# The ninth feature pair moves into the block products of the FFN down projection

## The chip, the cores and the metric

One core of a Trainium2 chip runs one encoder layer as one launch. The metric is device microseconds of an execution; the kernel before takes 2078.09 us (median of three runs, 2076.51 to 2078.81). The engines are TensorE (PE, matmuls; PEld is its weight load), VectorE (DVE), ScalarE (ACT), GpSimd (POOL) and SyncE (SP), which issues every load and store of the kernel on one queue. The 16 DMA engines carry them out.

## The reference, cut to what matters

```python
D_MODEL, SEQ, DEC_SEQ, D_FF = 1024, 1024, 32, 2816
def swiglu(h, w_gate, w_up, w_down):
    return (jax.nn.silu(h @ w_gate) * (h @ w_up)) @ w_down
def layer(x, lw, sb_fn, s0, gla_chunk):
    x = x + 0.5 * swiglu(rmsnorm(x, g_ffn1), w1g, w1u, w1d)
    mix, k, v, s = token_mixer(rmsnorm(x, g_mix), ...)
    x = x + mix
    x = x + 0.5 * swiglu(rmsnorm(x, g_ffn2), w2g, w2u, w2d)
    return rmsnorm(x, g_final), k, v, s
```

The prompt's 1024 rows and the sample's 32 are computed together: 1056 columns when x is held transposed. The change touches `@ w_down` of both FFNs, and what the gate/up stage hands to it.

## The kernel before, in words

Everything is held transposed: x is eight tiles x[0] to x[7] of 128 features by 1056 columns. Float32 operands are split into a high and a low float32r half, and each product is three matmuls (high x high, high x low, low x high). D_FF is 22 tiles of 128, taken as 11 pairs (0,1), (2,3), ... named 0 to 10.

**Block products.** Large products are done by a Strassen-Winograd scheme: operands are cut in 2x2 blocks, and seven products of sums of blocks replace eight. `PRODUCTS` names for each of the seven which weight form (A11, S2, ...) meets which moving form (B11, T2, ...) in which of four PSUM accumulators a to d; `ORDER` = (1, 6, 7, 5, 2, 4, 3) is the order in which they run. Products 5 and 3 share accumulator d, so VectorE must have read product 5's result before product 3 accumulates.

**Gate and up** (`gate_up`, L473 for its matmuls). Twenty steps t, two a pair, each of seven products. After each product the loop calls slots: `Slots.split` puts the copy to a high half (ACT, L50) and the subtraction of the low half (DVE, L51) in the slots k and k+1 later, and a store in slot k+2. The finished hidden pair lies in x[4] to x[7]. For the pairs that the block products of the down stage will use, `form` makes the seven moving forms out of it (B11, T1, T2 and so on; the T forms by a subtraction), and `keep` splits each in x[0] or x[1] in turn and stores it in the DRAM tensor `part_spill` (528 KB a form). Each pair's forms are spread over the two or three steps behind it. Pairs listed in `PLAIN` are stored unsplit in `hid_spill` or, if in `SPLIT`, split in `hid_split`.

**Down.** Two parts. `Down.strassen` runs groups of two pairs; a group has four steps (`DownStep`), one for each 256 output features, a step has seven products, and a product has 2 column quarters x 2 pairs x 3 matmuls of 264 columns (L822). Behind each product a result is added to x on VectorE (L811) and GpSimd (L840). Before: four groups, pairs 1 to 8. Moving operands come from `part_spill` into 14 places of h and X, two sets of 14 in turn. A step's weights are loaded raw, and `first` and `second` make the sums on GpSimd (L799 among them) and the splits. `Down.plain` then does the six tiles in `PLAIN` (pairs 0, 9, 10) as ordinary products, in three chunks of 352 columns in the first FFN and four of 264 in the second, with the next norm done beneath it (`mix_norm` and `final`).

**The hand-over.** `Down.head` runs in the last gate/up step (t = 19), product by product: it issues the loads of group 0's parts, of the first weights and of x[0] to x[3], which had been lent out as scratch (x[0] and x[1] for `keep`, x[2] and x[3] for other splits). x[4] to x[7] follow during steps 0 and 1.

**What sets the order.** On the five engines the order around the change is fixed by hand (`manual_schedule`) in these stages; SyncE is in order too. Each transfer counts on one of eight semaphores in turn, so an issue also waits for the transfer eight issues ahead.

## Time and profile before

| what | value |
|---|---|
| median of three runs | 2078.09 us (2076.51 to 2078.81) |
| time of the profiled execution | 2074.93 us |
| its span | 2073.1 us |
| mean granted TensorE clock | 0.947 |
| TensorE busy | 2030.5 us, 98% |
| VectorE, ScalarE, GpSimd busy | 67%, 43%, 32% |
| block products, first and second FFN | 481.2 to 647.6 us, 1825.6 to 1989.6 us |
| plain products, second FFN, start | 1990.4 us |

A line of the profile names the source line, the engine, the operation, the tile written and those read (`pd_d<-part,whl`), the shape, the count, the busy time and mean ns, and then in the idle time before it what ended that. Numbers of buffers are left out, so `part`, `h` and `x` each stand for several tiles. `x<-x` on SyncE is a load of x from the input in the first FFN, `x<-x_spill` the same in the second. A line of the stretch table gives the stretch, its length, then busy time and count for PE, PEld, DVE, ACT and POOL, then granted clock, DMA share and GB/s.

### The profile page before, as it was taken

To read this page: it belongs to the slowest core of one execution; us is meant where nothing else is said; L and a number is where in the kernel's file an instruction comes from. 1 tells how busy PE (TensorE), PEld (TensorE's weight loads), DVE (VectorE), ACT (ScalarE), POOL (GpSimd) and SP (SyncE) were. 2 spreads that over 40 slices of the span, in tenths; PEclk is the share of its full clock that TensorE was granted. 3 is DMA by queue.
4 is the path that set the end of the run, shared out by engine and by line. 5 is a ranking of instruction groups with operands and counts; after the bars stand their busy time and mean duration, and the time that the engine had idled before them with its cause. 6 is when DMAs were issued, how large, how long until landed. Compare 5 with 4: busy or idle time off the path is not lost.

```text
span 2073.1 us, 39052 instructions
## 1 busy us (share of the span) xinstructions
PE 2030.5 (98%) x15746; PEld 1975.2 (95%) x15746; DVE 1386.0 (67%) x2166; ACT 883.3 (43%) x1630; POOL 671.2 (32%) x554
## 2 busy tenths in 40 slices
PE   7999999999999999999999999999999999999998
PEld 6999999999999988988999998999999999999997
DVE  6877777765677657386555477695775666566654
ACT  6444444442223443336555575454443333322233
POOL 0144434436774200121222200002433343367720
PEclk9999999999999999999999999999999999999998
DMA  6267676769863111111314152332673333498631
GB/s 234 104 235 262 244 249 248 267 225 395 319 241 111 61 62 62 65 63 53 106 58 122 59 183 92 112 96 89 237 251 141 140 148 143 148 398 317 220 120 67
DMA packets 142132, 349.83 MB, mean 169 GB/s; under 512 B 13176, under 2 KB 37144, under 8 KB 138368
## 3 DMA queue, kind: packets, MB, share of 16 engines
q1 hardware_dynamic: 141376, 346.80, 46.9%
q8 instruction: 124, 2.03, 0.4%
q10 hardware_dynamic: 576, 0.54, 0.1%
q14 instruction: 56, 0.46, 0.1%
HBM read 216.96 MB, written 124.65 MB: 165 GB/s over the span
## 4 chain that ended last, share of the span: by engine, by line
PE 89%; DVE 5%; ACT 3%; DMA 1%; issue 1%; SPq 0%; POOL 0%; DVEq 0%; ACTq 0%
PE acc_a L473 11%; PE acc_c L473 11%; PE acc_d L473 11%; PE acc_b L473 6%; PE pd_d L822 4%; PE pd_a L822 4%; PE pd_c L822 4%; PE pj L118 4%; PE acc L381 4%; PE pj L119 4%; PE pj L120 4%; PE pd L118 2%; PE pd L120 2%; PE pd L119 2%; PE pd_b L822 2%; PE av L1652 2%
## 5 line engine op out<-in xcount | busy, mean ns | idle before, releaser
L473 PE MATMUL acc_a<-h,whl 128*128 128x264 f32 x1920 | 247.9, 285 | 0.3 <-DVE whl L51 0.3
L473 PE MATMUL acc_d<-part,S 128*128 128x264 f32 x1920 | 246.3, 284 | 0.0
L473 PEld LDWEIGHTS acc_a<-h,whl 128*128 128x128 f32 x1920 | 239.5, 189 | 0.5 <-DVE whl L51 0.5
L473 PEld LDWEIGHTS acc_d<-part,S 128*128 128x128 f32 x1920 | 238.5, 188 | 0.1
L118 PE MATMUL pj<-h,whl 128*128 128x352 f32 x576 | 203.0, 352 | 0.0
L120 PE MATMUL pj<-h,whl 128*128 128x352 f32 x576 | 188.7, 328 | 0.0
L119 PE MATMUL pj<-h,whl 128*128 128x352 f32 x576 | 187.7, 326 | 0.0
L51 DVE TENSOR_TENSOR x<-x 128x528 fp32r<-128x528 f32 (+1 forms) x188 | 155.8, 844 | 19.0 <-ACT x L50 19.0
L50 ACT ACTIVATE x<-x 128x528 fp32r<-128x528 f32 (+1 forms) x188 | 117.3, 634 | 119.5 <-DVE x L546 30.3
L526 POOL TENSOR_TENSOR x<-tc,x 128x528 f32<-128x528 f32 x60 | 100.3, 1672 | 184.2 <-DVE tc L525 147.2
L444 POOL TENSOR_TENSOR s<-wraw 128x512 f32<-128x512 f32 x38 | 60.9, 1601 | 230.1 <-DVE S L113 164.2
L473 PE MATMUL acc_c<-h,A 128*128 128x264 f32 x960 | 124.3, 285 | 0.6 <-DVE u L492 0.6
L473 PE MATMUL acc_b<-h,S 128*128 128x264 f32 x960 | 124.2, 285 | 0.0
L473 PE MATMUL acc_c<-part,S 128*128 128x264 f32 x960 | 123.1, 284 | 0.0
L473 PEld LDWEIGHTS acc_c<-h,A 128*128 128x128 f32 x960 | 120.4, 188 | 0.8 <-issue 0.8
L473 PEld LDWEIGHTS acc_b<-h,S 128*128 128x128 f32 x960 | 120.4, 188 | 0.0
L1628 DVE TENSOR_TENSOR_SCAN w<-f,w 128x128 f32<-128x128 f32 (+3 forms) x64 | 86.8, 1357 | 49.2 <-ACT w L1626 48.9
L473 PEld LDWEIGHTS acc_c<-part,S 128*128 128x128 f32 x960 | 119.3, 188 | 0.0
L1046 POOL TENSOR_TENSOR nr<-nv,mhalf 128x18 f32<-128x18 f32 (+1 forms) x15 | 46.3, 3086 | 219.2 <-DVE nv L1044 199.3
L118 PEld LDWEIGHTS pj<-h,whl 128*128 128x128 f32 x576 | 109.2, 190 | 5.5 <-issue 2.6
L51 DVE TENSOR_TENSOR S<-s,S 128x512 fp32r<-128x512 f32 x152 | 113.9, 750 | 0.6 <-ACT S L50 0.6
L840 POOL TENSOR_TENSOR x<-x,u 128x528 f32<-128x528 f32 x64 | 98.2, 1553 | 45.1 <-DVE x L811 45.1
(407 smaller groups left out, 4885.2 us busy)
## 6 DMA issues: line engine op xcount, KB each, us to landing
part_spill<-x SPq DMA_DIRECT2D x112, 528.0 KB, 3.8
h<-part_spill SPq DMA_DIRECT2D x64, 528.0 KB, 10.7
part<-part_spill SPq DMA_DIRECT2D x48, 528.0 KB, 10.8
win_split<-x SPq DMA_DIRECT2D x44, 512.0 KB, 3.4
whl<-win_split SPq DMA_DIRECT2D x22, 1024.0 KB, 5.0
wraw<-w1g SPq DMA_DIRECT2D x22, 512.0 KB, 5.2
wraw<-w1u SPq DMA_DIRECT2D x22, 512.0 KB, 6.1
x<-win SPq DMA_DIRECT2D x44, 256.0 KB, 3.0
```

The source lines that it names most:

```text
L50: self.later(k, lambda: nc.scalar.activation(hi, src, AF.Copy))
L51: self.later(k + 1, lambda: nc.vector.tensor_sub(lo, src, hi.bitcast(F32)))
L118: nc.tensor.matmul(out, w[:, 0, wsl], a[:, 0, asl], start=first, stop=False)
L119: nc.tensor.matmul(out, w[:, 0, wsl], a[:, 1, asl], start=False, stop=False)
L120: nc.tensor.matmul(out, w[:, 1, wsl], a[:, 0, asl], start=False, stop=last)
L381: nc.tensor.matmul(out, self.w[i](k, a), quarter(S, k, b, j), start=k == 0 and n == 0, stop=k == KT - 1 and n == 2)
L444: eng.tensor_add(self.s1, a21, a22)
L473: nc.tensor.matmul(t[:, s, :SW], w[:, a, ks], m(k, b, s), start=fresh and k == 0 and n == 0, stop=k == 3 and n == 2, skip_group_check=not ...
L526: nc.gpsimd.tensor_mul(two(hid), t, sg)
L822: nc.tensor.matmul(t[:, s, :SW], w[:, u, k * P : k * P + P], b[:, v, ss(s)], start=fresh and k == 0 and i == 0, stop=k == 1 and i == 2, sk ...
L840: nc.gpsimd.tensor_add(x[r][h], x[r][h], u)
L1628: nc.vector.tensor_tensor_scan(wr, f[:, :L][:, ::-1], wr, 0.0, op0=ALU.mult, op1=ALU.add)
```

## The change

Pair 9 (hidden tiles 18 and 19) leaves the plain list and joins the block products. Groups are now (1, 2), (3, 4), (5, 6, 7), (8, 9): group 2 has three pairs, so its products have 18 matmuls, and a step needs the weights of a third pair (`third`, `load_third`). The two sets of 14 places become a ring of 28, in which each group takes the places behind the group before it; a table made in `Down.__init__` says behind which product each part is loaded. The plain list keeps four tiles and four weight slabs instead of six and six. `form` stores seven forms of pair 9 where it stored four split halves, and since the last of them are now made in step t = 19, in x[0] and x[1], `head` loads x[0] ahead of part 6 and x[1] one product later.

```diff
@@ -525,18 +525,12 @@
                 nc.vector.tensor_add(t, u, ps)
                 nc.gpsimd.tensor_mul(two(hid), t, sg)
             f, h = 2 * self.i + q // 2, q % 2
-            if f in PLAIN and f not in SPLIT:
+            if f in PLAIN:
                 nc.sync.dma_start(S.hidden[PLAIN.index(f)][:, h * HALF : h * HALF + HALF], hid)
 
     def form(self, name):
 
         b11, b12, b21, b22 = (self.S.x[4 + q][:, :HALF] for q in range(4))
-        if 2 * self.i in SPLIT:
-            q = {"B11": 0, "T1": 1, "B21": 2, "B22": 3}.get(name)
-            if q is not None:
-                out = self.S.hid2[PLAIN.index(2 * self.i + q // 2)][:, :, q % 2 * HALF : q % 2 * HALF + HALF]
-                self.keep(out, self.S.x[4 + q][:, :HALF])
-            return
         if 2 * self.i in PLAIN:
             return
         if name[0] == "B":
...
@@ -763,9 +758,9 @@
 
 
 
-PAIRS = [(1, 2), (3, 4), (5, 6), (7, 8)]
-PLAIN = (0, 1, 18, 19, 20, 21)
-SPLIT = (18, 19)
+PAIRS = [(1, 2), (3, 4), (5, 6, 7), (8, 9)]
+THREE = 2
+PLAIN = (0, 1, 20, 21)
 
 
 class DownStep:
...
@@ -803,6 +798,29 @@
         self.W = {"A11": cut(self.wa, 0), "A12": cut(self.wa, 1), "A22": cut(self.wb, 0)}
         self.W.update({f"S{i + 1}": cut(self.ws, i) for i in range(4)})
 
+    def third(self, raw):
+
+        S, nc = self.S, self.S.nc
+        a11, a22, a21, a12 = (raw[:, i * P : i * P + P] for i in range(4))
+        wide, one = self.D.third
+        pair = self.wb[:, :, 2 * P :]
+
+        def sums():
+            nc.gpsimd.tensor_add(a22, a21, a22)
+            nc.gpsimd.tensor_sub(a21, a11, a21)
+            nc.gpsimd.tensor_sub(a11, a22, a11)
+
+        split = lambda w, src, k: S.slots.split(w[:, 0], w[:, 1], src, k)
+        cut = lambda t, i: t[:, :, i * P : i * P + P]
+        split(pair, raw[:, : 2 * P], 1)
+        S.slots.later(3, sums)
+        split(wide[:, :, : 3 * P], raw[:, : 3 * P], 4)
+        split(cut(wide, 3), a12, 5)
+        S.slots.later(7, lambda: nc.gpsimd.tensor_sub(a12, a12, a11))
+        split(one, a12, 8)
+        self.W3 = {"A11": cut(pair, 0), "A22": cut(pair, 1), "S4": one}
+        self.W3.update({n: cut(wide, i) for i, n in enumerate(("S2", "S1", "S3", "A12"))})
+
     def emit(self, between):
         S, nc = self.S, self.S.nc
         acc = {}
...
@@ -815,13 +833,15 @@
             if fresh:
                 acc[role] = S.ps.tile([P, 2, 512], F32, name="pd_" + role, tag="acc")
             t, w = acc[role], self.W[wn]
+            ks = len(PAIRS[self.g])
             for s in range(2):
-                for k in range(2):
+                for k in range(ks):
                     b = self.D.part(self.g, n, k)
+                    wk = w[:, :, k * P : k * P + P] if k < 2 else self.W3[wn]
                     for i, (u, v) in enumerate(((0, 0), (0, 1), (1, 0))):
                         nc.tensor.matmul(
-                            t[:, s, :SW], w[:, u, k * P : k * P + P], b[:, v, ss(s)],
-                            start=fresh and k == 0 and i == 0, stop=k == 1 and i == 2, skip_group_check=not fresh,
+                            t[:, s, :SW], wk[:, u], b[:, v, ss(s)],
+                            start=fresh and k == 0 and i == 0, stop=k == ks - 1 and i == 2, skip_group_check=not fresh,
                         )
             ps = t[:, :, :SW]
             if p == 1:
...
@@ -851,21 +871,40 @@
         h, X = S.h, S.X
         h0 = lambda d: h[d][:, :, :HALF]
         h1 = lambda d: h[d][:, :, HALF:]
-        self.places = [
-            [h0(0), h0(1), h0(2), h0(3), h1(0), h1(1), h1(2), h1(3)] + X[:6],
-            X[6:] + [h0(4), h0(5), h0(6), h0(7), h1(4), h1(5), h1(6), h1(7)],
-        ]
-        self.tiles = S.h[:4] + S.XX[:2]
+        self.ring = [f(d) for f in (h0, h1) for d in range(4)] + X + [f(d) for f in (h0, h1) for d in range(4, 8)]
+        self.base = [7 * sum(len(p) for p in PAIRS[:g]) for g in range(len(PAIRS))]
+        self.tiles = S.XX[: len(PLAIN)]
         self.ws = []
         self.steps = [DownStep(self, g, m) for g in range(len(PAIRS)) for m in range(4)]
-        self.raw = {}
+        self.raw, self.raw3 = {}, {}
+        self.loads = {}
+        for g in range(1, len(PAIRS)):
+            before, ks = len(PAIRS[g - 1]), len(PAIRS[g])
+            early = len(self.ring) - 7 * before
+            for i in range(7 * ks):
+                if i < early:
+                    m, n = divmod(i * 7 // min(early, 7 * ks), 2)
+                    n *= 2
+                else:
+                    m, n = 3, (i - early) // before + 1
+                self.loads.setdefault((4 * (g - 1) + m, n), []).append((g, *divmod(i, ks)))
 
     def part(self, g, n, k):
-        return self.places[g % 2][2 * n + k]
+        return self.ring[(self.base[g] + n * len(PAIRS[g]) + k) % len(self.ring)]
+
+    def load_one(self, g, n, k):
+        self.S.nc.sync.dma_start(self.part(g, n, k).bitcast(F32), self.S.parts[PAIRS[g][k] - 1, n])
 
     def load_part(self, g, n):
-        for k, i in enumerate(PAIRS[g]):
-            self.S.nc.sync.dma_start(self.part(g, n, k).bitcast(F32), self.S.parts[i - 1, n])
+        for k in range(len(PAIRS[g])):
+            self.load_one(g, n, k)
+
+    def load_third(self, i):
+        pool, name = (self.S.raw2, "wraw2") if i == 0 else (self.S.raw, "wraw")
+        t = pool.tile([P, 1024], F32, name=name, tag=name)
+        self.S.nc.sync.dma_start(t, self.src[len(self.steps) + i])
+        for m in range(2):
+            self.raw3[4 * THREE + 2 * i + m] = t[:, m * 512 : m * 512 + 512]
 
     def load_step(self, i):
         if i < len(self.steps):
...
@@ -888,10 +927,11 @@
             self.load_part(0, 5)
             self.steps[0].first(self.raw.pop(0), 1)
         elif p == 5:
+            self.S.nc.sync.dma_start(self.S.x[0], xd[0])
+            self.load_part(0, 6)
+            self.steps[0].second(1)
+        elif p == 4:
             self.S.nc.sync.dma_start(self.S.x[1], xd[1])
-            self.load_part(0, 6)
-            self.S.nc.sync.dma_start(self.S.x[0], xd[0])
-            self.steps[0].second(1)
         elif p == 3:
             self.load_step(2)
             for d in (2, 3):
...
@@ -923,14 +964,16 @@
                             self.steps[i + 1].first(self.raw.pop(i + 1), 1)
                         if n == 1:
                             self.steps[i + 1].second(2)
-                    if st.g < last and n % 2 == 0 and 4 * (n // 2) + st.m < 7:
-                        self.load_part(st.g + 1, 4 * (n // 2) + st.m)
+                        if n == 0 and self.steps[i + 1].g == THREE:
+                            self.steps[i + 1].third(self.raw3.pop(i + 1))
+                    for x in self.loads.get((i, n), ()):
+                        self.load_one(*x)
                     if (i, n) in at:
                         at[i, n]()
                     S.slots.now += 1
 
                 st.emit(between)
-            self.plain_slab(5)
+            self.plain_slab(3)
             while S.slots.at:
                 S.slots.run()
                 S.slots.now += 1
...
```

SyncE's issues at the hand-over in the first FFN, before. `part_352` are the two tiles of part 6 of group 0 (product 3's moving operand), L891 is x[1], L893 x[0], `hid_spill` the halves of pair 10; each row waits, by the semaphores in brackets, for the transfer eight rows ahead (DMAHW) and for the engine that last used the place:

```order
L529 DMA hid_spill<-x 128x528 [waits DMAHW2_49,Pool_49]
L891 DMA x<-x 128x1056 [waits DMAHW3_49]
L868 DMA part_352<-part_spill 128x2x528 [waits DMAHW4_49,PE_49]
L868 DMA part_352<-part_spill 128x2x528 [waits DMAHW5_49,PE_49]
L893 DMA x<-x 128x1056 [waits DMAHW6_49]
L529 DMA hid_spill<-x 128x528 [waits DMAHW7_49,DVE_49]
L529 DMA hid_spill<-x 128x528 [waits DMAHW0_49,Pool_49]
L529 DMA hid_spill<-x 128x528 [waits DMAHW1_49,Pool_49]
```

After, from the row behind the same hid_spill on. The first `part_spill` store is T2's (from x[0]), the second T4's (from x[1]); L930 is x[0], L934 x[1], L961 x[4], and `part_353` and `part_354` belong to group 1:

```order
L548 DMA part_spill<-x 128x1056 [waits DMAHW4_49,DVE_49]
L896 DMA part_353<-part_spill 128x2x528 [waits DMAHW5_49,PE_49]
L896 DMA part_353<-part_spill 128x2x528 [waits DMAHW6_49,PE_49]
L930 DMA x<-x 128x1056 [waits DMAHW7_49,DMAHW4_49]
L896 DMA part_352<-part_spill 128x2x528 [waits DMAHW0_49]
L896 DMA part_352<-part_spill 128x2x528 [waits DMAHW1_49]
L529 DMA hid_spill<-x 128x528 [waits DMAHW2_49,DVE_49]
L529 DMA hid_spill<-x 128x528 [waits DMAHW3_49,Pool_49]
L548 DMA part_spill<-x 128x1056 [waits DVE_49]
L961 DMA x<-x 128x1056 [waits DMAHW5_49,DMAHW2_49]
L896 DMA part_354<-part_spill 128x2x528 [waits DMAHW6_49,PE_49]
L934 DMA x<-x 128x1056 [waits DMAHW7_49,DMAHW4_49]
```

T2's store counts on DMAHW4 and x[0]'s load (L930) waits for it; T4's store counts on DMAHW4 as well, one round later, and x[1]'s load (L934) waits for that. T3's store stands ten rows ahead of T2's. Part 6 stood behind L891, which waited for its turn alone; it now stands behind L930, and two parts of group 1 stand ahead of that.

VectorE in step 0 of the down stage, before and after. The fourth row adds product 5 (`pd_d`) into x[1]:

```order
L811 SCALAR_TENSOR_TENSOR u_5640<-pd_b,s_5616 128x528 [waits DVE_49,PE_49,Activation_49]
L811 SCALAR_TENSOR_TENSOR tc<-pd_c,u_5640 128x528 [waits DVE_49,PE_49,Pool_49]
L51 TENSOR_TENSOR S_5622<-wraw,S_5622 128x512 [waits DMAHW0_49,Activation_49]
L811 SCALAR_TENSOR_TENSOR x<-pd_d,x 128x528 [waits DMAHW3_49,PE_49]
L51 TENSOR_TENSOR whl<-s_5618,whl 128x512 [waits Activation_49]
L811 SCALAR_TENSOR_TENSOR x<-pd_a,x 128x528 [waits DMAHW6_49,DMAHW2_49,PE_49]
```

```order
L829 SCALAR_TENSOR_TENSOR u_5655<-pd_b,s_5631 128x528 [waits DVE_49,PE_49,Activation_49]
L829 SCALAR_TENSOR_TENSOR tc<-pd_c,u_5655 128x528 [waits DVE_49,PE_49,Pool_49]
L51 TENSOR_TENSOR S_5637<-wraw,S_5637 128x512 [waits DMAHW0_49,Activation_49]
L829 SCALAR_TENSOR_TENSOR x<-pd_d,x 128x528 [waits DMAHW7_49,DMAHW4_49,PE_49]
L51 TENSOR_TENSOR whl<-s_5633,whl 128x512 [waits Activation_49]
L829 SCALAR_TENSOR_TENSOR x<-pd_a,x 128x528 [waits PE_49]
```

The order is unchanged; the fourth row waits for x[1]'s load, which is now DMAHW7.

More of the change, by code (lines that the diff above doesn't have):

```diff
@@ L901, in strassen @@
         S = self.S
-        last = len(PAIRS) - 1
-        todo = [(lambda n=n: self.plain_tile(n)) for n in range(12)]
+        todo = [(lambda n=n: self.plain_tile(n)) for n in range(2 * len(PLAIN))]
         at = {}
@@ L906, in strassen @@
             at[12 + n // 4, n % 4 * 2] = fn
-        for j, key in enumerate(((13, 1), (15, 0), (15, 1), (15, 2), (15, 3))):
+        for j, key in enumerate(((14, 0), (14, 3), (15, 1))):
             at[key] = lambda j=j: self.plain_slab(j)
+        for i, key in enumerate(((4 * THREE - 2, 1), (4 * THREE, 1))):
+            at[key] = lambda i=i: self.load_third(i)
+        self.third = S.sr.tile([P, 2, 512], F32R, name="S4", tag="S4"), S.s32.tile([P, 2, P], F32R, name="s3", tag="s3")
         E = mybir.EngineType
@@ L942, in plain_tile @@
         t = self.tiles[n // 2][:, :, cols]
-        if PLAIN[n // 2] in SPLIT or PLAIN[n // 2] < 2 and self.done is not None:
+        if PLAIN[n // 2] < 2 and self.done is not None:
             S.nc.sync.dma_start(t.bitcast(F32), S.hid2[n // 2][:, :, cols])
@@ L954, in plain_slab @@
         else:
-            pool, name = (S.raw, "wraw") if j in (0, 1, 3, 5) else (S.raw2, "wraw2")
+            pool, name = (S.raw, "wraw") if j < 2 else (S.raw2, "wraw2")
             raw = pool.tile([P, 1024], F32, name=name, tag=name)
-            S.nc.sync.dma_start(raw, self.src[len(self.steps) + j])
+            S.nc.sync.dma_start(raw, self.src[len(self.steps) + 2 + j])
             S.slots.split(w[:, 0], w[:, 1], raw, 3)
@@ L2072, in body @@
             down = Down(S, A["w2d"], A["w2d2"])
-            jobs = [(S.hidden[i], S.hid2[i]) for i in range(2)] + [(A["w2d"][16 + j], A["w2d2"][j]) for j in range(6)]
+            jobs = [(S.hidden[i], S.hid2[i]) for i in range(2)] + [(A["w2d"][18 + j], A["w2d2"][j]) for j in range(4)]
             splits = Splits(S, halves_of(jobs), (S.x[2], S.x[3]))
@@ L2142, in down @@
                 for r, half in ((0, 0), (0, 1), (1, 1), (1, 0)):
-                    blocks += [tile(2 * i + half, 2 * m + r) for i in g]
+                    blocks += [tile(2 * i + half, 2 * m + r) for i in g[:2]]
             out += [np.concatenate(blocks[n : n + 8], 1) for n in range(0, len(blocks), 8)]
+        blocks = [tile(2 * PAIRS[THREE][2] + half, 2 * m + r) for m in range(4) for r, half in ((0, 0), (1, 1), (1, 0), (0, 1))]
+        out += [np.concatenate(blocks[n : n + 8], 1) for n in range(0, len(blocks), 8)]
         blocks = [w[f * P : f * P + P, m * 256 : m * 256 + 256] for m in range(4) for f in PLAIN]
```

14 lines of the change are left out of this document (7 added, 7 removed).

## The prediction

> **What bounds the kernel now.** I read the page's busy times first, then TensorE's waits in the two down stages, then SyncE's issues in time around the start of each down stage, since all loads and stores go through that one queue.
>
> ```profile
> PE 2030.5 (98%) x15746; PEld 1975.2 (95%) x15746; DVE 1386.0 (67%) x2166; ACT 883.3 (43%) x1630; POOL 671.2 (32%) x554
> PE pd_d L822 <- DVE whl L51: 1.4, 1, 1.4
> PE pd_d L822 <- DMA part<-part_spill: 0.6, 1, 0.6
> PE pd L118 <- DVE x L811: 0.8, 1, 0.8
> ```
>
> TensorE is busy 98% of the span, so matmuls are the bound and a matmul removed is time saved. The next two rows are all of its waits in the first FFN's down stage (470 to 660 us), the last is the only one in the second FFN's (1800 to 2000 us). Both rows of the first are at one spot, product 3 (the seventh) of step 0, where the down stage has just begun:
>
> ```profile
> 487.02 1.63 PE L822 MATMUL pd_a<-part,S 128*128 128x264 f32 x12
> 488.49 1.62 PE L822 MATMUL pd_c<-part,S 128*128 128x264 f32 x12
> 491.52 0.60 PE L822 MATMUL pd_d<-part,whl 128*128 128x264 f32 x3 [1.41 <-DVE whl L51]
> 493.95 1.63 PE L822 MATMUL pd_a<-h,S 128*128 128x264 f32 x12
> 490.08 0.71 DVE L811 SCALAR_TENSOR_TENSOR x<-pd_d,x 128x528 f32<-128x528 f32 x1 [2.96 <-DMA x<-x]
> ```
>
> Product 3 accumulates into `pd_d`, which VectorE must first have added into x[1] (product 5). VectorE sat 2.96 us waiting for x[1] to be loaded. So the end of this stage hangs on when x[1] and the last parts arrive, and that is set by SyncE's queue:
>
> ```profile
> 473.13 4.75 SPq L868 DMA_DIRECT2D part<-part_spill  x4
> 478.38 0.73 SPq L529 DMA_DIRECT2D hid_spill<-x  x1
> 479.69 0.33 SPq L891 DMA_DIRECT2D x<-x  x1
> 481.11 1.90 SPq L868 DMA_DIRECT2D part<-part_spill  x2
> 483.85 0.33 SPq L893 DMA_DIRECT2D x<-x  x1
> 485.24 3.15 SPq L529 DMA_DIRECT2D hid_spill<-x  x3
> 490.00 1.72 SPq L898 DMA_DIRECT2D x<-x  x2
> 473.00:476.00 3.00, 3.00 (x27) 3.00 (x26) 0.77 (x2) 0.00 (x0) 2.63 (x3) 0.95 1.04 405
> 1814.00:1817.00 3.00, 3.00 (x27) 3.00 (x26) 0.70 (x1) 0.42 (x1) 0.00 (x0) 0.95 1.03 403
> part<-part_spill SPq DMA_DIRECT2D x7, 528.0 KB, 10.7
> hid_spill<-x SPq DMA_DIRECT2D x4, 264.0 KB, 9.1
> part_spill<-x SPq DMA_DIRECT2D x112, 528.0 KB, 3.8
> ```
>
> The two window rows (last figures: DMA share, GB/s) show the 16 DMA engines full at about 400 GB/s: one 528 KB transfer (541 kB) takes 1.35 us. In the window 467 to 493 us a transfer takes 10.7 us from issue to landing, and even a 264 KB **store** 9.1 us, while over the whole program a 528 KB store has a median of 3.8. The queue is served in order with eight transfers in flight (8 x 1.35 = 10.8). x[1], issued at 479.69, landed at 490.08.
>
> **The change part by part.**
>
> *Matmuls.* Per FFN, pair 9 leaves the plain products: two of six hidden tiles. The second FFN loses 4 x 8 x 2 x 3 = 192 matmuls of 264 columns, the first 3 x 8 x 2 x 3 = 144 of 352. Each gains 7 x 4 x 2 x 3 = 168 block matmuls of 264.
>
> ```profile
> 481.18 1.62 PE L822 MATMUL pd_a<-h,S 128*128 128x264 f32 x12
> 482.64 1.62 PE L822 MATMUL pd_b<-h,whl 128*128 128x264 f32 x12
> 648.08 0.32 PE L118 MATMUL pd<-h,part 128*128 128x352 f32 x1
> 649.53 0.32 PE L118 MATMUL pd<-part,whl 128*128 128x352 f32 x1
> ```
>
> Starts lie 1.46 us apart for 12 matmuls of 264 (0.122 each), and 1.45 us for the nine from the third row to the fourth (0.161 each, 352 columns). Second FFN: 24 x 0.122 = 2.9. First: 144 x 0.161 - 168 x 0.122 = 2.7. **Term 1: -5.6 us.**
>
> *The new stores ahead of the reloads.* Pair 9's forms T3, T2, T4 are now made in the last gate/up step and stored from x[1], x[0], x[1]. SyncE's order then makes x[0]'s reload wait for T2's store to have landed, and x[1]'s for T4's; before, neither waited for a store. While SyncE stands there nothing behind it is issued: product 3's own parts (`part_352`), hid_spill, T4's store, x[4]. First FFN, in order at 1.35 us each (0.67 for hid_spill), issue being held by the transfer eight places ahead:
> - T3's store takes the place in the queue that landed at 478.4 (hid_spill's issue of 478.38 waited for it). The eight parts behind it land one place later, the last at 489.2; hid_spill 489.9.
> - T2's store is issued at 481.1 and lands at 491.3, behind them. Two parts of group 1 behind it land at 494.0.
> - x[0] is issued at 491.4, lands 495.4; `part_352` 496.7 and 498.0; two hid_spills 498.7 and 499.4; T4's store 500.7.
> - x[4] waits for the first of those hid_spills and is issued at 498.8; an idle queue takes some 3.8 us, so it lands at about 502.5, one part at 503.9. x[1], issued at 500.8 after T4, lands at 505.2 instead of 490.08.
>
> Product 3 followed x[1] by 491.52 - 490.08 = 1.44 us: 506.6. Its 12 matmuls take 1.46, so step 1 begins at 508.1, not at 493.95: **+14.1 us**. Behind it wait x[2], x[3] (four places later, about 510) and group 1's parts (wanted at 538): no second stop.
>
> The second FFN has the same order:
>
> ```profile
> 1819.14 0.35 SPq L529 DMA_DIRECT2D hid_spill<-x  x1
> 1830.05 0.33 SPq L874 DMA_DIRECT2D wraw<-w2d  x1
> 1831.32 1.72 SPq L898 DMA_DIRECT2D x<-x_spill  x2
> 1834.37 1.62 PE L822 MATMUL pd_d<-part,whl 128*128 128x264 f32 x12
> 1835.82 1.63 PE L822 MATMUL pd_a<-h,S 128*128 128x264 f32 x12
> ```
>
> The load at 1830.05 waited for hid_spill, eight places ahead; the next, at 1831.32, for x[1]. With T3's place that hid_spill lands at 1831.4, T2's store at 1832.8, x[0] 1836.8, the two parts 1839.5, T4's store 1842.2, x[1] 1846.4. Product 3 starts at 1847.8 instead of 1834.37: **+13.4 us**. **Term 2: +27.5 us.** Bounds: if a store lands 3.8 us after issue, as in an unfilled queue, x[1] is there some 7 us earlier in each FFN (about +14 in all); if SyncE loses 3 us more at each (transfers that start only when the queue is empty), +33. I take the queue's own row, 9.1 to 10.7 us, since the stores enter a full queue.
>
> The Trainium skill, "DMA: Bandwidth & Descriptors", section Queues, rings and completion order, says that descriptors are consumed in ring order but completion is not first-in first-out. By the second half a store might pass, and the sum would be the bound of +14; by the row, a hid_spill in this full queue took 9.1 us, so ring order decides.
>
> *TensorE after the stop.* Its longest wait in these stages is 1.4 us; now it stands some 16 us twice. What long idling does is seen only at the ends of this program:
>
> ```profile
> 2066.00:2070.00 4.00, 0.00 (x0) 0.00 (x0) 2.19 (x6) 0.17 (x1) 1.45 (x2) 0.50 0.52 176
> 22.00:24.00 2.00, 2.00 (x10) 2.00 (x10) 1.61 (x3) 0.45 (x1) 0.00 (x0) 1.00 1.02 408
> 24.00:26.00 2.00, 2.00 (x18) 2.00 (x18) 0.69 (x1) 2.00 (x4) 0.00 (x0) 0.95 1.06 314
> ```
>
> With no matmul, at the end, the granted clock (third figure from the right) is 0.50. At the start, after 9 us of nothing, TensorE fully busy does 10 matmuls in 2 us until 24 us, then 18. So a restart is at about half rate for a while: between nothing and 12 us x 45% = 5.4 us lost at each stop. I take 2.5: **term 3, +5 us** (0 to +10.8). The Trainium skill, "TensorE: Matmul & The Clock Gate", section What's actually happening, has the clock halved after an idle window of about 3.4 us and restored after a busy one; an estimate by it is 1.7 to 3.4 us a stop, 3.4 to 6.8 in all.
>
> *The plain stage's cover.* Its column chunks shrink by a third, while the norms done beneath them do not.
>
> ```profile
> 671.00:694.00 23.00, 23.00 (x141) 22.78 (x140) 15.85 (x29) 10.23 (x19) 4.58 (x4) 0.95 0.16 56
> 694.00:718.00 24.00, 24.00 (x149) 23.77 (x148) 17.20 (x32) 9.70 (x20) 6.76 (x9) 0.95 0.18 61
> 2027.00:2045.00 18.00, 18.00 (x149) 17.93 (x148) 10.28 (x27) 7.91 (x20) 0.00 (x0) 0.95 0.18 61
> ```
>
> A chunk of the first FFN is now 8 x 12 x 0.161 = 15.5 us of TensorE over 15.9 to 17.2 us of VectorE (third time): VectorE leads. In the second FFN 11.7 stand over 10.3 with a burst of multiplications in it, and the last chunk's lag reaches the end. Bounds: nothing, or all of term 1 (5.6). **Term 4: +2.5 us.**
>
> *Costed at nothing.* The four extra subtractions and three splits per FFN, 0.7 us of VectorE each: it is busy 0.77 of 3 us in the 473 row; uncovered, 5 us per FFN. The third pair's weights (four additions of 128x128 on GpSimd and four small splits a step), and seven more parts for group 2 (7 x 1.35 = 9.5 us):
>
> ```profile
> 522.00:563.00 41.00, 41.00 (x339) 41.00 (x338) 28.14 (x42) 11.46 (x21) 31.77 (x30) 0.95 0.85 316
> ```
>
> Four steps of 10.25 us leave GpSimd 2.3 us a step and DMA 15%; group 2's own steps grow to 15.4 us with the same sums. Uncovered in step 7 alone, under 1 us.
>
> **Sum.** -5.6 + 27.5 + 5 + 2.5 = +29.4 us, on the profiled execution's span of 2073.1 (time 2074.93): 2102.5. The median of the runs is 2078.09, so 2107.5; I say **2107**.
>
> **The rivals.**
> - *The reloads are hidden (other side).* If both x reloads land before VectorE wants them (490 and 1831.6), only terms 1 and 4 are left: -3.1, at best -5.6: 2072.5 to 2075. It decides if the stores land within about 3 us of each other and T4's enters the queue before 482. For it: a store alone takes 3.8 us. Against it: SyncE is in order, and the reload behind T2 stands ahead of T4's store.
> - *Half the price.* Stores land in 3.8 us: -5.6 + 14 + 3 + 2.5 = +14, 2092. For it: the queue drains while SyncE stands. Against it: T2's store enters it full.
> - *Worse.* The clock stays halved for 12 us at each stop and VectorE takes the whole plain gain: -5.6 + 27.5 + 10.8 + 5.6 = +38, 2116.
> - *No effect to be seen.* About 4 us of new wait against term 1: 2078.
>
> **How the numbers follow.** Forecast 0.66 (own range 2098 to 2113), half price 0.13, worse 0.12, hidden 0.06, no effect 0.03. The range reaches from the half price's 2088 to the worst case's 2116. Differences under 0.2% (4 us) cannot be told from none: faster 0.06, same 0.03, slower 0.91.
>
> **What would show it.** In the changed profile: a wait of TensorE of 12 us or more at product 3 of step 0 in both FFNs, put down to VectorE, and behind that to x's load; SyncE's queue standing some 7 us before each x[0] load; a granted clock under 0.95 just after; fewer `pd` matmuls (384 and 288 instead of 576 and 432), more block ones. If x[1] lands by 492 and 1833, the forecast is wrong.

## The result, and the profile after

The changed kernel takes **2116.12 us** (median of 4 runs, 2110.94 to 2116.41), the kernel before 2078.45 (4 runs beside them, 2076.51 to 2080.59). The ratio is 1.0168, 95% interval 1.0145 to 1.0191: 1.7% slower. The profiled execution took 2116.06 with a span of 2114.28; before it was 2074.93 and 2073.12, so the profiled pair is 41.2 us apart.

The busy times of the page, then TensorE's waits (two of 0.8 and 0.6 us in the last window are left out), first in 470 to 660 us (most of the first FFN's block products), then 660 to 760 (their end, the plain products and the first projections), then 1840 to 2110 (the second FFN's down stage); columns are total, number and longest:

```profile
PE 2034.6 (96%) x15746; PEld 1978.3 (94%) x15746; DVE 1398.9 (66%) x2206; ACT 890.7 (42%) x1662; POOL 684.2 (32%) x586
...
PE pd_d L842 <- DVE x L829: 17.9, 1, 17.9
...
PE st L146 <- DVE acc L145: 2.8, 2, 1.6
PE pj L120 <- DVE whl L113: 1.5, 1, 1.5
...
PE pd_d L842 <- DVE x L829: 17.0, 1, 17.0
```

TensorE now stands 17.9 and 17.0 us at one place in each FFN. The instructions in order of time on TensorE and VectorE show which, and what is behind it:

```profile
508.23 3.01 PE L842 MATMUL pd_d<-part,whl 128*128 128x264 f32 x12 [17.89 <-DVE x L829]
511.03 2.23 PE L842 MATMUL pd_a<-h,S 128*128 128x264 f32 x12
513.10 1.13 PE L842 MATMUL pd_b<-h,whl 128*128 128x264 f32 x8
1875.89 3.01 PE L842 MATMUL pd_d<-part,whl 128*128 128x264 f32 x12 [17.04 <-DVE x L829]
1878.70 2.70 PE L842 MATMUL pd_a<-h,S 128*128 128x264 f32 x12
1881.24 1.64 PE L842 MATMUL pd_b<-h,whl 128*128 128x264 f32 x12
507.46 0.71 DVE L829 SCALAR_TENSOR_TENSOR x<-pd_d,x 128x528 f32<-128x528 f32 x1 [20.21 <-DMA x<-x]
1875.13 0.71 DVE L829 SCALAR_TENSOR_TENSOR x<-pd_d,x 128x528 f32<-128x528 f32 x1 [19.27 <-DMA x<-x_spill]
```

It is product 3 of step 0; VectorE's addition into x[1] waited some 20 us for x[1]'s load. SyncE's issues around it, first FFN and then second (L548 is a store of T2 or T4, L930 x[0], L961 x[4], L934 x[1]):

```profile
480.79 0.33 SPq L548 DMA_DIRECT2D part_spill<-x  x1
482.16 1.89 SPq L896 DMA_DIRECT2D part<-part_spill  x2
491.00 0.34 SPq L930 DMA_DIRECT2D x<-x  x1
...
494.32 0.64 SPq L548 DMA_DIRECT2D part_spill<-x  x1
499.75 0.33 SPq L961 DMA_DIRECT2D x<-x  x1
...
501.76 0.33 SPq L934 DMA_DIRECT2D x<-x  x1
...
1847.09 0.33 SPq L548 DMA_DIRECT2D part_spill<-x  x1
...
1857.29 0.33 SPq L930 DMA_DIRECT2D x<-x_spill  x1
...
1860.03 0.43 SPq L548 DMA_DIRECT2D part_spill<-x  x1
...
1869.06 0.32 SPq L934 DMA_DIRECT2D x<-x_spill  x1
```

T2's store is issued at 480.79, SyncE has nothing more to do from 484.05 (482.16 + 1.89), and x[0]'s load goes out at 491.00, when the store has landed: 6.95 us of standing. Only behind that comes T4's store, and only behind its landing x[1]. By the trace, T2's stores landed at 490.98 and 1857.28 us and T4's at 501.74 and 1869.05; the loads of x[0] and x[1] were issued within 0.02 us of these landings.

Where the 41.2 us are, by the starts of TensorE's matmuls in both profiles. "Hand-over" is the time from step 0's first block product to step 4's, so all of group 0 is in it; "attention" runs from the last low-rank product to the second FFN's first block product, and no matmul in it was changed:

| stretch | before | after | difference |
|---|---|---|---|
| first FFN: hand-over | 43.47 | 61.02 | +17.55 |
| first FFN: step 4 to the last plain product | 193.83 | 193.07 | -0.76 |
| from there to the first low-rank product | 8.46 | 11.68 | +3.22 |
| attention and the second gate/up stage | 1075.65 | 1079.83 | +4.18 |
| second FFN: hand-over | 40.93 | 60.54 | +19.61 |
| second FFN: step 4 to the last plain product | 195.27 | 192.48 | -2.79 |

They add to +41.0. The two hand-overs hold 37.2 of it. The second gate/up stage takes 409.73 us in both profiles, so the +4.18 lies in the attention alone.

### The profile page after: what moved, and what is told of

Its sections match the earlier page's. It is cut to its first block, busy times and chain, and to the rows that moved or that the text cites. A ratio compares the mean times of both kernels' runs of the same rounds, so it can differ in the third digit from the quotient of the medians.

```text
span 2114.3 us, 39205 instructions
## 1 busy us (share of the span) xinstructions
PE 2034.6 (96%) x15746; PEld 1978.3 (94%) x15746; DVE 1398.9 (66%) x2206; ACT 890.7 (42%) x1662; POOL 684.2 (32%) x586
## 4 chain that ended last, share of the span: by engine, by line
PE 85%; DVE 7%; DMA 4%; ACT 3%; issue 1%; SPq 0%; DVEq 0%; ACTq 0%
PE acc_a L473 11%; PE acc_c L473 10%; PE acc_d L473 10%; PE acc_b L473 5%; PE pd_d L842 5%; PE pd_a L842 5%; PE pd_c L842 5%; PE pj L118 4%; PE acc L381 4%; PE pj L119 4%; PE pj L120 4%; PE pd_b L842 2%; DMA part_spill<-x 2%; PE av L1695 2%; PE po L118 1%; PE po L120 1%
## 5 line engine op out<-in xcount | busy, mean ns | idle before, releaser
L50 ACT ACTIVATE x<-x 128x528 fp32r<-128x528 f32 (+1 forms) x190 | 118.7, 634 | 142.5 <-DMA part_spill<-x 41.2
```

The source lines that it names most:

```text
L50: self.later(k, lambda: nc.scalar.activation(hi, src, AF.Copy))
```

## The experiments

All twelve are told; medians with the kernel before beside them:

| run | median us | before | ratio, 95% interval |
|---|---|---|---|
| e1 scratch elsewhere | 2085.35 | 2078.75 | 1.0030, 1.0017 to 1.0043 |
| e2 T4 alone | 2085.36 | 2078.75 | 1.0026, 1.0013 to 1.0039 |
| e2 T2 alone | 2102.82 | 2078.75 | 1.0116, 1.0087 to 1.0144 |
| e3 kernel before with the stores | 2112.98 | 2078.75 | 1.0162, 1.0138 to 1.0187 |
| e4 norms to GpSimd | 2086.14 | 2077.43 | 1.0047, 1.0031 to 1.0064 |
| e5 hand-over in the ring | 2083.66 | 2077.43 | 1.0027, 1.0014 to 1.0039 |
| e6 e4 and e5 | 2092.05 | 2077.43 | 1.0061, 1.0044 to 1.0077 |
| e7 norms later | 2087.31 | 2078.21 | 1.0049, 1.0035 to 1.0064 |
| e8 queue order | 2105.42 | 2078.21 | 1.0125, 1.0104 to 1.0147 |
| e9 slab place | 2091.82 | 2077.70 | 1.0062, 1.0040 to 1.0083 |
| e10 all of it | 2094.25 | 2077.70 | 1.0073, 1.0059 to 1.0086 |
| e11 less for VectorE | 2083.63 | 2075.01 | 1.0040, 1.0024 to 1.0056 |

Single runs of one kernel lie up to 15 us apart with the granted clock (last section), so small effects are read from the stretches of the profiles. A hand-over that stops TensorE also holds what the halved clock behind the stop costs:

| stretch | before | after | e1 | e2 T4 | e2 T2 | e3 | e5 | e8 | e10 |
|---|---|---|---|---|---|---|---|---|---|
| first hand-over | 43.47 | 61.02 | 47.58 | 47.60 | 54.70 | 61.86 | 45.98 | 52.41 | 50.57 |
| second hand-over | 40.93 | 60.54 | 45.14 | 44.61 | 53.90 | 58.86 | 43.82 | 53.26 | 46.90 |

**Which wait is it?** Theory A is the prediction's: SyncE stands for T2's and T4's stores before it issues the reloads. Rival B is the added traffic, rival C the block or plain stage itself. Four runs tell them apart. The first moves the scratch:

```diff
-        t = S.x[S.n_kept % 2].bitcast(F32R)...
+        t = S.x[{62: 2, 63: 3}.get(S.n_kept, S.n_kept % 2)].bitcast(F32R)...
...
-            self.S.nc.sync.dma_start(self.S.x[0], xd[0])
+            self.S.nc.sync.dma_start(self.S.x[1], xd[1])
             self.load_part(0, 6)
+            self.S.nc.sync.dma_start(self.S.x[0], xd[0])
             self.steps[0].second(1)
-        elif p == 4:
-            self.S.nc.sync.dma_start(self.S.x[1], xd[1])
```

> The changed kernel, with T2 of pair 9 stored from x[2] and T4 from x[3] instead of x[0] and x[1], and x[1], part 6, x[0] loaded in the order of the kernel before. The same bytes go through the same queue; only whose store a reload waits for is changed. Theory A (SyncE stands for T2's and T4's stores before it issues x[0] and x[1], and product 3 of step 0 waits behind that): the 17.7 and 19.6 us at the two hand-overs go, bar 1 to 3 us each for the stores' own places in the queue, so 2079 to 2086 us; TensorE's wait at that product falls from 17.9 and 17.0 us to under 5. Rival B (it is the added traffic, three more stores of 528 KB per FFN in a full queue, that makes x[1] late, whatever it waits for): x[1] is as late as before, 2105 to 2116. Rival C (the block stage with a group of three pairs, or the plain stage, loses the time): 2105 or more too, with product 3 early.

TensorE's waits in the two hand-overs of this run:

```profile
PE pd_d L842 <- DVE whl L51: 3.2, 1, 3.2
PE pd_d L842 <- DMA part<-part_spill: 0.6, 1, 0.6
...
PE pd_d L842 <- DMA part<-part_spill: 2.2, 2, 1.5
```

The waits of 17.9 and 17.0 us are gone; the hand-overs fall by 13.4 and 15.4 us. The same bytes go through the same queue and the block and plain stages are as in the changed kernel, so neither B nor C is behind these. The run also brings back the old order of the loads; but in the changed kernel each of the two loads left as its store landed (see above), so it was the stores that held them.

What is left of the change is +6.6 us (2085.35 against 2078.75, and 6.6 in the profiles too): 4.1 and 4.2 at the hand-overs, where 1 to 3 each were expected, less 1.8 over the other stretches. The stores still take places in the queue ahead of x[1], part 6 and then x[3], so this rest is what B can still claim. Of the first 4.1 us, 1.8 are more waiting at product 3 (3.2 + 0.6 against 1.4 + 0.6) and 1.6 the halved clock behind it.

The second moves T4 alone (`{63: 3}`, order x[1], part 6, x[0]), the third T2 alone (`{62: 2}`, order of the changed kernel, in which x[1] is loaded two products behind x[0], as product 2 stands between 5 and 4 in `ORDER`).

> As the run above, but T4 alone goes elsewhere (x[3]); T2 is still stored from x[0]. Order x[1], part 6, x[0]. Theory A: x[1] waits for no new store and lands by about 491; only x[0]'s load stands for T2 until about 491 and lands at 495 to 497, where the addition of product 2 (the fifth) needs it, so step 1 begins 2 to 5 us later than in the run above in each FFN: that run plus 4 to 10 us, 2083 to 2096. Rival B: 2105 to 2116.

> T2 alone goes elsewhere (x[2]); T4 is still stored from x[1]; order of the changed kernel (x[0], part 6, and x[1] two products later). Theory A: T4's store is no longer held up behind x[0]'s reload, is issued at about 485 and lands at about 495; x[1] is issued then and lands at 499 to 500 instead of 507: product 3 some 8 to 10 us later than in the first run, in each FFN, plus about 1 us of halved clock: that run plus 16 to 22 us, 2096 to 2106. Rival B: 2105 to 2116.

In the run with T2 alone moved TensorE waits, in the first FFN and in the second:

```profile
PE pd_d L842 <- DVE x L829: 11.7, 1, 11.7
PE pd_d L842 <- DVE x L829: 10.2, 1, 10.2
```

T4 alone does as much as both: hand-overs of 47.60 and 44.61 against 47.58 and 45.14. The expected 2 to 5 us for x[0] behind T2's store did not come; by step 4 nothing is left of them. T2 alone leaves hand-overs 7.1 and 8.8 us longer than the first run's, and by the medians 17.5 us in all, where theory A said 16 to 22. So the 17.6 and 19.6 us have three parts: 4.1 and 4.2 that stay with both stores moved; 7.1 and 8.8 for x[1] behind T4's store; and 6.3 and 6.6 more when T2's store comes first, since x[0]'s reload behind it holds T4's store back.

> The kernel before with nothing of the change but the late stores: pair 9's T3, T2 and T4 are formed, split and stored from x[1], x[0], x[1] to a place in DRAM that nobody reads, and x[0], x[1] are reloaded in the changed kernel's order. Plain products, groups and loads of group 1 stay as before. Theory A: the hand-over loss by itself, +17 to +20 us in each FFN, 2112 to 2118. Rival C (group of three pairs or plain stage): under 2083, since neither is there. Rival B (traffic) expects the same as A here; the first run tells it apart.

```diff
+            else:
+                src, x, y = {"T3": (b12, b22, b12), "T2": (b22, b22, b11), "T4": (b21, b21, b22)}[name]
+                self.S.nc.vector.tensor_sub(src, x, y)
+                self.keep(self.S.parts[self.i - 1, PARTS.index(name)], src)
```

(`n_kept` starts at 0 in each FFN, and x[0], x[1] are reloaded in the changed kernel's order.) The kernel before, given nothing but these stores, waits like the changed one, in the first FFN and the second:

```profile
PE pd_d L827 <- DVE x L816: 18.6, 1, 18.6
PE pd_d L827 <- DVE x L816: 16.0, 1, 16.0
```

+18.4 and +17.9 us at the hand-overs, 2112.98 in all: the disputed cost by itself, with neither the group of three pairs nor the shorter plain stage.

**What eats the plain stage's gain?** In the first FFN 2.7 us of matmuls were saved, only 0.76 is left at the stage's end, and 3.22 is lost behind it. Term 4 said that VectorE has more to do than a chunk now covers. First (e4), four more of the norm's subtractions a chunk go to GpSimd (on the kernel of the first run, as in all of this part):

```diff
-        split_to(S, S.h[d][:, 0, cs(c)], S.h[d][:, 1, cs(c)], t, d % 2 == 1)
+        split_to(S, S.h[d][:, 0, cs(c)], S.h[d][:, 1, cs(c)], t, pool or d % 2 == 1)
```

> The first run (scratch in x[2] and x[3], 2085 us, span 2079.7 in the profile) with one edit in the first FFN's plain stage: in column chunks 0 and 1 of the norms all eight subtractions that form h's low half are GpSimd's instead of four. Forecast's term 4 (VectorE leads when a chunk of TensorE has 15.5 us over it): 8 x 0.68 = 5.4 us leave VectorE, so most of the 4.8 us between the plain stage and the first q product (1.6 of the matmuls' gain lost within the stage, 3.2 behind it) come back, 2 to 4.5 us below the first run. Rival (a chain, not a load: the last chunk's sums, norm and splits, which are not touched): within 1 us of the first run, or slower, as GpSimd takes 1.15 us for what VectorE does in 0.68.

No gain came: from step 4 to the first low-rank product it is 208.5 us against 204.8 in the first run, and still some 206 without the two half-clock stretches that fall into it (an estimate by 1.3 us each, last section). VectorE's groups in 672 to 738 us, first run and then this one (columns: busy us, mean ns):

```profile
L168 DVE SCALAR_TENSOR_TENSOR hf<-x,gains,rs_y 128x352 f32<-128x352 f32 x23 | 14.3, 669 | 0.9 <-POOL h L111 0.8
L145 DVE TENSOR_TENSOR acc<-acc,sq 128x352 f32<-128x352 f32 x21 | 11.4, 542 | 5.3 <-ACT sq L140 4.4
```

```profile
L168 DVE SCALAR_TENSOR_TENSOR hf<-x,gains,rs_y 128x352 f32<-128x352 f32 x19 | 16.0, 896 | 1.0 <-POOL h L111 0.8
L145 DVE TENSOR_TENSOR acc<-acc,sq 128x352 f32<-128x352 f32 x21 | 12.8, 611 | 5.1 <-ACT sq L140 4.6
```

VectorE's own instructions grew longer while GpSimd subtracted: 896 ns instead of 669 for `hf`, 611 instead of 542 for `acc`. That is 19 x 0.23 + 21 x 0.07 = 5.8 us put on VectorE for the 5.4 taken off, so the run does not decide about VectorE's load. Taken one by one between 672 and 740 us, the 9 `hf` that no GpSimd subtraction overlapped took 580 ns on average and the 12 that one overlapped 1078; in the first run it was 18 at 577 and 6 at 931. The Trainium skill, "SBUF — State Buffer", section SBUF: two separate sides, says that a VectorE instruction with two SBUF inputs and a GpSimd instruction that reads SBUF share one pair of ports, which the first to start holds for its whole length; these durations agree.

The second try (e7) emits the norm one feature tile later (`if c and d == 2`), so that 36 matmuls stand ahead of the statistics' matmul again, as before the change.

> The first run (2085 us) with one edit in the plain stage of both FFNs: the norm of the chunk before is emitted after the third feature tile of a chunk (36 matmuls with two pairs) instead of the second (24; with three pairs the second was 36). Theory for what is left of term 4 (a chain whose cover shrank: last sums, squares, additions of a chunk, then the statistics' matmul that stands in TensorE's own order): the waits at that matmul, 2.8 us in two places in the first run, go to under 0.5 and the plain stage of the first FFN ends 1.5 to 2.5 us earlier against its start; the 3.2 us behind the stage (a projection weight late on VectorE) stay: 2082 to 2084 us by the same clock. Rival (VectorE's load): the wait moves to another matmul, no gain.

```profile
PE pj L120 <- DVE whl L113: 3.5, 1, 3.5
PE st L146 <- DVE acc L145: 0.8, 1, 0.8
```

The wait at the statistics falls from 2.8 to 0.8 (under 0.5 was expected), but the one at the q product grows from 1.5 to 3.5: the rival's outcome. Stage and gap (from the first plain product to the last, and on to the first low-rank one) take 62.2 us against 61.0, one half-clock stretch among them. The third (e9) asks whether the q weight is late because of its buffer. In the change slabs 2 and 3 lie in the two `whl` buffers, in the kernel before 1 and 5; slab 1 is free earlier:

```diff
-            at[key] = lambda j=j: self.plain_slab(j)
+            at[key] = lambda j=j: self.plain_slab((0, 2, 1)[j])
...
-        w = S.wp.tile(...) if j > 1 else S.XX[len(PLAIN) + j][:, :, :1024]
+        w = S.wp.tile(...) if j % 2 else S.XX[len(PLAIN) + j // 2][:, :, :1024]
```

> The first run (2085 us; in its profile 11.7 us from the last plain matmul to the first low-rank one, 8.5 in the kernel before) with one edit: of the four weight slabs of the plain products, slabs 1 and 3 lie in the two whl buffers and 0 and 2 in the part tiles, as slabs 1 and 5 did in the kernel before; in the changed kernel it is 2 and 3. New theory: the first q weight takes the whl buffer that is free first; before, slab 1 was done after feature tile 3 of the last chunk (its copy on ScalarE at 705.7, 13 us ahead of the stage's end), now slab 2 only after tile 5 (718.8, 3 us ahead), so its subtraction comes late on VectorE. It expects the copy 5 us or more earlier, the wait at the q product gone and 2 to 3.2 us less behind the plain stage: 2081 to 2083 by the same clock. Rival (VectorE's load, term 4 as forecast): under 0.5 us.

The q weight's copy on ScalarE and its subtraction on VectorE, in the kernel before, the first run and this run (their last plain matmuls start at 718.48, 721.91 and 723.44):

```profile
705.66 1.05 ACT L109 ACTIVATE whl<-wraw 128x1024 fp32r<-128x1024 f32 x1
712.31 1.96 DVE L113 TENSOR_TENSOR whl<-wraw,whl 128x1024 fp32r<-128x1024 f32 x1
```

```profile
718.77 1.05 ACT L109 ACTIVATE whl<-wraw 128x1024 fp32r<-128x1024 f32 x1
722.43 1.53 DVE L113 TENSOR_TENSOR whl<-wraw,whl 128x1024 fp32r<-128x1024 f32 x1
```

```profile
716.20 1.05 ACT L109 ACTIVATE whl<-wraw 128x1024 fp32r<-128x1024 f32 x1
724.39 1.83 DVE L113 TENSOR_TENSOR whl<-wraw,whl 128x1024 fp32r<-128x1024 f32 x1
```

The copy is 7.2 us ahead of the stage's end instead of 3.1, but the subtraction still comes 0.95 us behind it: it stands in VectorE's order behind the norm of chunk 1. TensorE's wait at the q product is 2.2 us, not gone. The way to the low-rank product is 12.40 us against 11.71, and some 11.1 without the one half-clock stretch in it: 0.6 less, where 2 to 3.2 were expected. The buffer is not the main cause; that theory fell. So the last run of this part (e11) takes the work off VectorE and gives it to nobody (`cut` holds for chunks 0 and 1):

```diff
+        if cut and d % 2 == 0:
+            nc.scalar.activation(S.h[d][:, 0, cs(c)], t, AF.Copy)
+            continue
```

> The first run (profile: 49.3 us from the first to the last plain matmul of the first FFN, 11.7 from there to the first low-rank one, waits of 2.8 at the statistics and 1.5 at the q product) with VectorE's four subtractions for h's low half left out in the norms of column chunks 0 and 1 (the low half of four of the eight feature tiles keeps old data, so what follows computes on other numbers; nothing is given to GpSimd in their place). 8 x 0.68 = 5.4 us leave VectorE. Term 4 as forecast (VectorE has more work than a chunk of TensorE's covers): the q weight's subtraction, at 722.4 in the first run, comes 3 us or more before the stage's end, the wait at the q product goes, and stage and gap together shrink from 61.0 to 57 to 59 us. A chain that VectorE's load does not set: 60 us or more. By the whole time 2 to 4 us below the first run at the same clock.

TensorE's only wait in 660 to 760 us is now

```profile
PE pj L120 <- DVE whl L113: 0.6, 1, 0.6
```

and stage and gap shrink from 61.0 to 57.2 us (47.45 + 9.72), within the 57 to 59 expected. From step 4 to the last plain product it is 191.26 us against 193.83 before, -2.57: term 1's -2.7 is there as soon as VectorE lets it through. That VectorE's load eats the gain is shown for the stage. Behind it, 2.0 of the 3.2 us come back; the q weight's subtraction starts at the stage's end (722.17 against 722.19), not 3 us ahead of it, and 1.3 us of the gap stay unexplained.

**Can the hand-over be mended?** The other runs tried to get what the first run left, and so a version that beats both. The ring run (e5) puts T2 and T4 into the two ring places that are used last, stores them in step 0, and loads x[1] ahead of the last parts:

```diff
+        late = S.n_kept - 62
+        if late < 0:
+            t = S.x[(S.n_kept + 1) % 2]...
+        else:
+            t = S.h[2 + late][:, :, :HALF]
...
+        if late >= 0:
+            S.slots.later(8 - late, store)
```

> The changed kernel with another hand-over: T2 and T4 are split into the two ring places that are filled last (in use again three steps later) and stored in step 0, behind every load that step 0 needs; T3 and T1 change places, so x[1], wanted first, waits for the older store and is loaded ahead of the last parts. Theory A with the queue's order as price (each 528 KB transfer ahead of x[1] and the last part costs 1.35 us): the first run's remaining 4.2 us in each FFN go, and the 2.0 us that the kernel before itself waits at product 3 of the first FFN: 8 to 11 us below the first run, 2074 to 2078 us, about the kernel before. If the rest of the first run's loss is the block stage's own, no gain against it: 2083 to 2086.

> Both edits on the changed kernel. If theory A and term 4 hold, the gains add: 2070 to 2075 us, faster than the kernel before by 0.2% or more (matmul term -5.6, the removed wait -2, and half a dozen tenths left behind the plain stage). If only the hand-over's holds: 2074 to 2078.

TensorE's waits in the first hand-over of the ring run:

```profile
PE pd_c L849 <- DMA part<-part_spill: 2.0, 2, 1.4
PE pd_d L849 <- DMA h<-part_spill: 1.3, 1, 1.3
```

No wait for x is left here, but TensorE waits for the parts themselves. The hand-overs are 45.98 and 43.82, still +2.5 and +2.9 on the kernel before: 8 to 11 us below the first run were expected, 3 came. The run with both edits was expected at 2070 to 2075 us and took 2092.05. Its profile is 2.0 us longer than the ring run's, with 2.5 more between step 4 and the first low-rank product, where the GpSimd edit is (one half-clock stretch is in it); its other runs took longer still at a granted clock of 0.989 to 0.994.

The last two take every store out from ahead of the reloads: T3 and T1 change places, x[1] is loaded between parts 4 and 5, T2 and T4 are stored from x[2] and x[3] behind x[0]'s load. The first (T2 from x[3], T4 from x[2]) also moves pair 10's `hid_spill` and the loads of x[4] to x[7] back; the second (T2 from x[2], T4 from x[3]) leaves those nearly as they were and has the slabs of the run above. Both have the later norms.

> The changed kernel with a hand-over that takes all stores out from ahead of the reloads: T3 and T1 change places and x[1] is loaded between parts 4 and 5; T2 is split into x[3] and T4 into x[2] and both are stored behind x[0]'s load; pair 10's four hid_spill stores move into step 0; x[4] to x[7] are loaded one step later; and the norm as in the run beside this. If what is left at the hand-over is only the bytes ahead of x[1] and the last part (1.35 us for each 528 KB, 0.67 for each hid_spill), step 1 starts 12.0 to 13.0 us after step 0 in both FFNs (10.25 at best; 12.8 and 10.2 in the kernel before, 15.1 and 13.2 in the first run), x[3] may cost 1 to 2 us in step 1, and the time is 2074 to 2080, level with the kernel before or 0.2% under it. If the queue cannot give the parts sooner whatever the order, 2081 to 2084.

```diff
+        t = S.x[{62: 3, 63: 2}.get(S.n_kept, (S.n_kept + 1) % 2)]...
+        S.slots.split(t[:, 0], t[:, 1], src, 1, None if S.n_kept == 62 else store)
+        if S.n_kept == 62:
+            S.slots.later(5, store)
...
+                S.slots.later(4, spill) if f > 19 else spill()
...
-                    if i < 2 and n in (1, 3):
-                        d = 4 + 2 * i + n // 2
+                    if i in (1, 2) and n in (1, 3):
+                        d = 2 + 2 * i + n // 2
```

> The queue order of the run of 2105 us with what was late there put back: x[4] to x[7] are loaded in steps 0 and 1 again and the hid_spill stores go in their old places behind x[0] (only the first waits for one product); T2 goes to x[2] and T4 to x[3]; norms one feature tile later; slabs as in the run beside this. If the waits found so far are all of the loss: step 1 some 11 to 12 us after step 0 (12.8 and 10.2 before), nothing more to step 4, half of term 1's gain in the first FFN and all of it in the second: 2071 to 2077 us, at or under the kernel before. If x[2] and x[3] are late behind T2's and T4's stores, 2 us more in each FFN.

```diff
+        t = S.x[{62: 2, 63: 3}.get(S.n_kept, (S.n_kept + 1) % 2)]...
...
+                S.slots.later(1, spill) if q == 3 else spill()
```

Step 1 starts 11.3 us after step 0 in the first FFN of the first of them (12.77 in the kernel before, 29.72 in the changed one), so the wait at product 3 of step 0 can be removed. But x[3]'s load then stood for T2's store (issued at 496.02), everything behind it went out late, and step 2 paid. SyncE's loads of x[3] and x[2] (L941) and x[5] (L964), and VectorE's addition into x[5]:

```profile
496.02 1.57 SPq L941 DMA_DIRECT2D x<-x  x2
511.17 0.33 SPq L964 DMA_DIRECT2D x<-x  x1
520.64 0.71 DVE L833 SCALAR_TENSOR_TENSOR x<-pd_d,x 128x528 f32<-128x528 f32 x1 [6.90 <-DMA x<-x]
```

x[5], issued at 511.17, was wanted at 513.7; TensorE stood 7.6 us in the first FFN and 9.1 in the second. With x[4] to x[7] in their old places it was 3.0 in each, and the hand-overs were still 7.1 and 6.0 us longer than before. 2074 to 2080 and 2071 to 2077 us were expected; 2105.42 and 2094.25 came. Each of these tries moved the wait to the next reload behind a store. None of the versions beats the kernel before.

## Why the prediction came out right

The direction, the place and the chain of causes were right; the size was too small. The time (2107) was 9 us under the median, which lies above the forecast's own range (2098 to 2113) and at the very end of the whole one (2116; its lower end of 2088 is 4 us under the half price's 2092 and is not worked out). The forecast's +29.4 stands against +37.7 by the medians and +41.2 in the profiled pair, in which the terms are read one by one:

- **Term 1, matmuls: -5.6.** Second FFN: -2.79 where -2.9 was worked out. First: -2.57 of -2.7 once VectorE is out of the way (the run with less for VectorE). The rates held.
- **Term 2, stores ahead of the reloads: +27.5; measured +32.8** (the hand-overs' +37.2 less the 4.4 of term 3). T2's part was right to 0.3 us: its store was to land at 491.3, and x[0] went out at 491.00. Ring order decided: T2's store of 528 KB, issued into the full queue, took 10.2 us in each FFN, as the rows of 9.1 and 10.7 had it, and the half price at 3.8 us was out. The step that was too small is the next one, "x[1], issued at 500.8 after T4, lands at 505.2". From x[0]'s issue to x[1]'s the working has 9.4 us in each FFN; it took 10.8 (491.00 to 501.76) and 11.8 (1857.29 to 1869.06). x[1]'s own load has 4.4 and 4.2; it took 5.6 (to 507.4) and 6.0 (to 1875.1). What the step left out is that the queue moves fewer bytes while SyncE stands and starts again:

```profile
500.00:504.00 4.00, 0.00 (x0) 0.00 (x0) 0.00 (x0) 0.00 (x0) 0.00 (x0) 0.50 0.99 292
1865.00:1869.00 4.00, 0.00 (x0) 0.00 (x0) 0.00 (x0) 0.00 (x0) 0.00 (x0) 0.50 0.66 239
508.00:511.00 3.00, 2.77 (x12) 2.78 (x13) 3.00 (x6) 0.00 (x0) 1.77 (x2) 0.50 1.02 414
```

  The last figure of the first two rows is 292 and 239 GB/s. From x[0]'s issue to x[1]'s landing the mean is 306 GB/s in the first FFN and 296 in the second, against 393 and 397 in the 17 us ahead, and not the 400 by which the landings were counted. The DMA share, one figure before, fell to 0.66 in the second row but not in the first (0.99), so idle DMA engines are only a part of it; the rest stays open. The bound of +33, which had 3 us more for each restart of the queue, is where it came out.
- **Term 3, the halved clock: +5; measured +4.4.** After the stop 12 matmuls took 2.80 us and the next 12 2.07 (508.23, 511.03, 513.10) instead of 1.46 each: 1.9. In the second FFN 2.81 and 2.54: 2.4. The granted clock of 0.50 stands in the last row above. The estimate by the Trainium skill, "TensorE: Matmul & The Clock Gate", section What's actually happening, 1.7 to 3.4 us a stop, agrees. The price hardly grows with the stop: in the first run a wait of 3.2 + 0.6 us was followed by a half-clock stretch too, and the next 21 matmuls took 4.19 us (494.58 to 498.77) instead of 2.56, 1.6 lost.
- **Term 4, the plain stage's cover: +2.5; measured +5.2** (1.9 within the first FFN's stage, 3.2 behind it, 0.1 in the second FFN), near the upper bound of 5.6. Mechanism right, size wrong: the forecast looked for it at the chunks and the program's end and did not follow VectorE's order to the next stage's first weight, which stands behind the norms.
- **Costed at nothing.** The extra splits, the third pair's weights and group 2's loads did cost nothing: between the hand-over and the plain stage TensorE has no wait in either FFN, and the second gate/up stage, where forms of pair 9 are made, takes 409.73 us as before. What the sum did not foresee is **+4.2 in the attention**, which the change does not touch (last section).

By these: -5.6 + 32.8 + 4.4 + 5.2 + 4.2 = 41.0.

The rival "reloads hidden" needed T4's store in the queue before 482; it went in at 494.32, behind x[0], as its counter-argument said. "Worse" has the right total, 2116, and was right that VectorE takes nearly the whole plain gain (5.2 of 5.6). But the clock was not halved for 12 us of work at each stop (4.4 us against 10.8); 5.3 us more for the queue and the attention's 4.2 stand in its place, so that its total fits is luck. What the prediction named as its signs all came: a wait over 12 us put down to VectorE and x's load in both FFNs, 6.95 us of standing ahead of x[0] in each (from 484.05 and 1850.34), a clock of 0.50 behind it, 288 and 384 `pd` matmuls.

## What to carry to other kernels

Where a buffer is both scratch for a store and the target of the next load in an in-order queue, the load pays the store's whole way through the queue (10.2 us for T2's store in the full queue here, 7.4 and 9.0 for T4's), and so does everything issued behind it; choose scratch whose next load is not wanted soon, and order the buffers so that the first one wanted waits for the oldest store. When work is taken from the leading engine, divide what the other engines do under it by the new, shorter time, and follow the overrun in their order to the first thing the next stage needs. Count a restarted queue at the rate it has then, not at its full rate.

## What the runs showed of the hardware that was not expected

**Half-clock stretches without a long idle.** The clock record of every trace has stretches of 3.41 us (or several together) at 0.50 in the attention, where TensorE's longest wait is 2.6 us. This is several together, in the slab run e9 (third figure from the right is the clock):

```profile
875.00:880.00 5.00, 5.00 (x37) 4.97 (x38) 1.84 (x5) 4.94 (x6) 1.18 (x1) 0.98 0.00 0
880.00:890.00 10.00, 10.00 (x39) 10.00 (x39) 7.54 (x10) 4.57 (x7) 0.76 (x2) 0.50 0.00 1
```

37 matmuls in 5 us, then 39 in 10. How many there are differs from run to run, and the attention's time goes with it: one stretch in five profiles, 1074.2 to 1075.9 us; two, 1076.6; three, 1078.5; four, 1077.7 and 1080.9; five, 1079.8 and 1080.4; six, 1082.7; seven, 1082.8; nine, 1086.2. A straight line through all fourteen has 1.3 us a stretch, and single profiles lie up to 1.6 us off it. The changed kernel's five against one would make 5.4; the +4.2 measured is that within the scatter. Whole runs follow it too: the kernel before took 2073.3 us at a mean clock of 0.998 and 2088.6 at 0.991. Why one run has more of them stays open. The Trainium skill, "TensorE: Matmul & The Clock Gate", section What's actually happening, says that the window by which activity is judged runs free of the program; that would fit, but no run here shows it.

**A clock that says little.** Outside the half-clock stretches the kernel before was granted 0.949 through its profiled execution, the changed one 1.000, and twelve matmuls of 264 columns took 1.46 us in both.

**GpSimd slows VectorE.** One VectorE instruction form took 580 ns without a GpSimd subtraction beside it and 1078 with one, 896 instead of 669 in the mean once more of them were moved there, so moving work gave nothing back.
